# AdaLN's second and third parts in branch B's product and wo's, and key pages loaded ahead of q's loop

## The chip, the cores and the metric

The kernel runs on one core of one Trainium2 chip. Its metric is the device time of one launch in microseconds. Of the kernel before there are three timed runs and one execution that was profiled.

## The reference, cut to what matters

One layer of a decoder for a prompt of 512 tokens and 8 samples with one token each, with D = 1024, 16 heads, and a past of 1024 positions a sample in pages of 128 (float32 throughout):

```python
sh1, sc1, g1, sh2, sc2, g2 = split(silu(c) @ ada_w + ada_b, 6)     # adaLN
h = rms_norm(x, norm1_g) * (1.0 + sc1) + sh1
xr, gr, q, k, v, fl, ga, gb = split(h @ w_in)
ya = (rg_lru(causal_dwconv(xr)) * gelu(gr)) @ w_proj_a             # branch A
yb = attend(q, k, v, log_sigmoid(fl + b_f)) @ w_proj_b             # branch B
x = x + g1 * ((sigmoid(ga) * ya + sigmoid(gb) * yb) @ w_o)
h2 = rms_norm(x, norm2_g) * (1.0 + sc2) + sh2
x = x + g2 * ((silu(h2 @ w_gate) * (h2 @ w_up)) @ w_ffn_out)
y = rms_norm(x, normf_g)
```

For a sample, `attend` takes the logits of q against the keys of its own pages, adds the sums of the logarithms of the forget gates between the two positions, and takes a softmax over past and present together. The page table gives each sample's pages; the product with the keys is what the change moves the loads of. `ada_w` is 1024 x 6144, 24 MB, and its six outputs are needed at different times: sh1 and sc1 for h, g1 only after wo, sh2 and sc2 for h2, g2 at the end.

## The kernel before, in words

Tokens lie along the free dimension (520 columns: 512 of the prompt, 8 samples), in two halves of 260; features lie on the partitions in eight tiles of 128. A product of 128 outputs runs over eight tiles of the inputs, and each step is three matmuls: high part of the weights by high part of the input, low by high, high by low. So a half of a product is 24 matmuls and a whole one 48.

Weights come through `wraw` (two buffers of 1 MB, loaded by SyncE in `load_chunks`, 256 columns at a time), and `split_upto` makes their high part on ScalarE (`whi`, L246) and their low part on VectorE (`wlo`, L248), three buffers of each. `begin()` opens a product: it calls `tick`, loads chunks and splits weights some products ahead. `tick` runs the work on the samples' past: it sums key pages (`key_sum`), and issues the loads of the next ones (`key_pages`, as many as the table `KEYS` says for that product). Each engine runs its instructions in a fixed order, which a list scheduler chose; `tc.issue_after` puts one instruction behind another.

A key page for the first samples comes in halves. `key_halves` takes one buffer of the pool `pgp` (seven buffers, shared with AdaLN's weights and the value pages) and has GpSimd issue two loads of 256 KB (`page_load`, L698, each with a read of the page table before it at L697, and at least four loads behind the last). The row of q by which the page is multiplied (`qb`, L715) is broadcast by another load from GpSimd; it comes from `qtd`, which ScalarE stores after the first four products of q were transposed. `key_sum` is a multiply (L742) and a reduce (L743) on VectorE.

AdaLN is computed in three parts. The first (scale and shift of h) is done at the start. The second (g1, sh2) and the third (sc2, g2) are each made of eight pieces, one for each tile of the inputs: `ada_load` (L350 and following; two loads of 512 KB, `araw`) and `ada_piece` (four matmuls at L370 with 32 output columns each, in the four column groups of the array). `ada_copy` takes the sum out of the bank, and `ada_end` transposes it (four transposes at L382) and adds the bias on VectorE.

The order of the stages: AdaLN's first part and h; q's loop (eight products; before the change a piece of AdaLN's second part follows each but the first); the RG-LRU loop (xr, gates A and B, gr, with the eighth piece); k, v and the prompt's attention; branch A's product (pa); branch B's product in the merge loop (pb), into which the table `ADA2` puts four pieces of the third part; wo by halves (`wo_done`, four more pieces in its first half); then the FFN. Before wo's product SyncE also loads x again (L100) and, tile by tile, the sigmoids and branch A (`sB`, `tA`), which are added and multiplied to `mix`. In q's loop there are further the past's forget gates: `past_load` gathers them, `past_turn` transposes them (eight transposes) and sums them on GpSimd (L451 to L454); and the weights of the RG-LRU's gates are split (`gate_split`, L909 and L910).

Of the kernel before, what the change touches and what calls it, by code (L numbers as in the profile page):

```python
# [12 lines left out]
ALU = mybir.AluOpType  # L13
# [5 lines left out]
NP = 512  # L19
NS = 8  # L20
# [45 lines left out]
def kernel(ctx, tc, xT, par, gates, b_f, cst, cse, own, cache_k, cache_v, cache_lf, pt,  # L66
# [13 lines left out]
    def slot(name, cols=NT, dt=F32, parts=128):  # L80
        return heap.tile([parts, cols], dt, name=name, tag="slot")
# [108 lines left out]
    def flush():  # L190
        while stores:
# [1 line left out]

    later = {}

    KEYS = dict(zip(range(42), (2, 2, 1, 0, 2, 2, 2, 2, 1, 1, 1, 1, 2, 2, 2, 1, 0, 1, 0, 1, 2, 2, 2, 2, 1, 1, 1, 1, 2, 2, 1, 2,
                                1, 1, 1, 2, 1, 1, 1, 1, 2, 0)))
    VALUES = (19, 21, 23, 25, 27, 29, 31, 35, 37, 39)
    LAST_POOL = 41
# [152 lines left out]
    def ada_load(which, kq):  # L352
        if kq >= KT:
            return
        for g2 in range(2):
            raw = pgp.tile([128, 2, 512], F32, name="araw", tag="pg")
            c0 = which * 2048 + g2 * 1024
            sp.dma_start(raw, ada_w[kq * 128:kq * 128 + 128, c0:c0 + 1024].rearrange("p (g c) -> p g c", g=2))
            ada_raw.setdefault((which, kq), []).append(raw)
# [13 lines left out]
    def ada_copy(which):  # L373
        sb = slot("adas", 512)
        act.copy(sb, ada_acc[which])
        ada_acc[which] = sb
# [54 lines left out]
    def past_load():  # L431
        t = wp.tile([NS * NPAGE, 2048], F32, name="lfp", tag="wraw", bufs=2)
        pool.indirect_dma_start(out=t, out_offset=None, in_=cache_lf,
                                in_offset=bass.IndirectOffsetOnAxis(ap=idx[:, 0:1], axis=0),
                                bounds_check=NPOOL - 1)
        lfp.append(t.rearrange("p (k h) -> p h k", h=H))
# [70 lines left out]
    def first_h(f):  # L507
        t, hi, lo = slot("hr"), slot("hh", dt=F32R), slot("hl", dt=F32R)
        a_, b_ = amp1[:, f, 0:1], mod[:, 0, f, 0:1]
        act.activation(hi[:, :NP], xn[f][:, :NP], AF.Identity, scale=a_, bias=b_)  # L510
        pool.tensor_tensor(t[:, NP:], xn[f][:, NP:], amp1[:, f, 1:9], ALU.mult)
        pool.tensor_tensor(t[:, NP:], t[:, NP:], mod[:, 0, f, 1:9], ALU.add)
        dve.tensor_scalar(t[:, :NP], xn[f][:, :NP], a_, b_, ALU.mult, ALU.add)
        act.copy(hi[:, NP:], t[:, NP:])
        dve.tensor_tensor(lo, t, hi.bitcast(F32), ALU.subtract)
        h.append((hi, lo))
# [76 lines left out]
    q_weights(1, raw, 4, 2)  # L593
    raw = wraw()
    q_weights(1, raw, 0, 4)
    for n in range(3):
        ada_load(1, n)
    load_chunks(0)
    sp.dma_start(cs[:, C_TRI:], cst[:, C_TRI:])

# [33 lines left out]
    def forget_logits(w):  # L634
        part, fl = slot("flp", parts=2 * H), slot("fl", parts=H)
        for j, (t0, t1) in enumerate(HALVES):
            b = bank(f"pfl{j}")
            for k in range(KT):
                for m in range(2):
                    pe.matmul(b[:2 * H, :HALF], lhsT=w[:, k], rhs=h[k][m][:, t0:t1],  # L640
                              start=k == 0 and m == 0, stop=k == KT - 1 and m == 1)
            act.copy(part[:, t0:t1], b[:2 * H, :HALF])

        def close():
            for j, (t0, t1) in enumerate(HALVES):
                b = bank(f"pfs{j}")
                pe.matmul(b[:H, :HALF], lhsT=cs[:2 * H, C_S16:C_S16 + H], rhs=part[:, t0:t1], start=True, stop=True)
                act.activation(fl[:, t0:t1], b[:H, :HALF], AF.Identity, bias=bf)
            sp.dma_start(fld, fl)

        return close
# [55 lines left out]
    def key_halves(s, j, half):  # L707
        if not S:
            S.extend(slot("S", 512) for _ in range(2))
        pg = pgp.tile([128, 2, 512], F32, name="pg", tag="pg")  # L710
        for a in range(2):
            page_load(cache_k, s, j + a, pg[:, a], 512 * half, 512 * half + 512)
        if j == 0:
            t = slot("qb", 512)
            pool.dma_start(t, qtd[s:s + 1, 512 * half:512 * half + 512].partition_broadcast(128))  # L715
            qb[0] = t
        pend.append([0, s, j, pg, qb[0], half])

    def key_page(s, j, half=None):
# [155 lines left out]
    q8 = keep.tile([128, KT * NS], F32, name="q8")  # L875

    def q_done(i, t):
        pool.tensor_copy(q8[:, NS * i:NS * i + NS], t[:, NP:])
        sp.dma_start(qd[i], t)
        pe.transpose(qtp[i // 4][:, 128 * (i % 4):128 * (i % 4) + 128], t[:, NP:], ident)  # L880
        if i % 4 == 3:
            q_samples(i // 4)
# [30 lines left out]
    for i in range(KT):  # L913
        if i % 4 == 0:
            qtp.append(bank(f"qt{i}", NS))
        if i < 6:
            t = qpart[i]
            for j, (t0, t1) in enumerate(HALVES):
                b = bank(f"q{i}_{j}")
                for k in range(4):  # L920
                    q_matmuls(1, i, j, k, b)
                dve.tensor_tensor(t[:, t0:t1], b[:, :HALF], t[:, t0:t1], ALU.add)
        else:
            t = slot("q")
            product(f"q{i}", h, to(t, act.copy))
        if ready:
            q_done(*ready.pop())
        ready.append((i, t))
        if i == 2:
            flw = forget_weights()  # L930
        if i == 3:
            split_upto(0)
            for n in range(KT):
                gate_load(n)
        if i >= 4:
            for n in (2 * i - 8, 2 * i - 7):
                gate_split(n)
        if i == 4:
            past_load()
            split_upto(1)  # L940
            with tc.issue_after(state["last"].ins), tc.issue_after(state["act"].ins):
                decay()
                past_conv()
            close = forget_logits(flw)
        if i == 6:
            close()
            past_turn(0)
        if i == 7:
            past_turn(1)
        if i:  # L950
            ada_piece(1, i - 1)
            if i < 5:
                ada_load(1, i + 2)
        if i == 3:
            q_done(*ready.pop())
        if i == 5:
            tick(2, 0)
    q_last = ready.pop()


# [105 lines left out]
    for i in range(0, KT, 2):  # L1066
        conv(i)
        if i == 0:
            q_done(*q_last)
        else:  # L1070
            if i == 2:
                ada_piece(1, 7)
                ada_copy(1)
            both(lru_root, i - 2)
            gelu(i - 2)
            lru_scan(i - 2)
        conv(i + 1)
        if i:
            gelu(i - 1)
            lru_scan(i - 1)  # L1080
            if i < 6:
                both(lru_mul, i - 2)
                both(lru_g, i - 2)
        if i < 6:
            gate_a(i)
            if i:
                lru_gates(i)
            gate_a(i + 1)
            if i == 2:
                ada_end(1)  # L1090
            lru_gates(i + 1 if i else 0)
            gate_b(i)
            if i == 0:
                lru_gates(1)
                past_sums(0)
            gate_b(i + 1)
            if i == 0:
                past_sums(1)
                ada_load(1, 7)
            both(lru_exp, i)  # L1100
            if i == 2:
                log_forget()
            if i == 4:
                sum_forget()
        else:
            lru_gates(i)
            with tc.issue_after(state["gate"].ins):
                both(lru_mul, i - 2)
                both(lru_g, i - 2)
                split_upto(state["n"] + 2)  # L1110
            gate_a(i)
            lru_gates(i + 1)
            gate_a(i + 1)
            both(lru_exp, i)
            gelu(i)
            both(lru_root, i)
            gelu(i + 1)
            both(lru_scan, i)
            both(lru_mul, i)
            both(lru_g, i)  # L1120
# [317 lines left out]
        dve.tensor_tensor(t, t, u, ALU.add)  # L1438
        mix[i] = split("mix", t)

    ADA2 = [(0,), (), (1,), (), (2,), (), (3,), (), (4,), (5,), (6,), (7,), (), (), (), ()]
    for i in range(KT):
        if i == 6:
            load_x()
        if i + 1 < KT:
            merge_load(i + 1)
        merge(i)
        for n in ADA2[i]:
            ada_piece(2, n)
    amp2 = []  # L1450


# [67 lines left out]
                    split_upto(u + KT + i)  # L1520

    def wo_done(i, j, b):
        for n in ADA2[KT + i] if j == 0 else ():
            ada_piece(2, n)
            if n == KT - 1:
                ada_copy(2)
        if i == 6 and j == 0:
            ada_end(2)
            amp2.append(amplitude("n2", 4, P_N2))
        residual(i, b, 2, j)  # L1530
        sum_squares("sq2", i, ss2, x[i], j, pool if i < 6 else dve)
# [243 lines left out]
```

## Time and profile before

| | us |
|---|---|
| three runs, median (lowest, highest) | 1024.76 (1024.56, 1027.04) |
| the profiled execution | 1028.43 |
| its span, first to last instruction | 1026.5 |
| TensorE busy in it | 998.2 |
| VectorE busy | 797.3 |
| ScalarE busy | 548.3 |
| GpSimd busy | 323.9 |

The span is what the profile shows of one execution; the time has a little around it (1.9 us here). Busy shares are means over stages with different limits, so what counts is, at each place, which engine is waited for. Rows of the timeline begin with the start in us and the duration; a duration of a matmul is modelled, so the distance between starts is what a matmul costs. `x8` at the end of a row counts records. In brackets stands how long the engine idled before the row and what it waited for. A name with a q behind the engine (SPq) is the issuing of a transfer.

### The profile page before, as it was taken

The numbers are of one execution on the slowest core, as the hardware profiler recorded it, in microseconds if no ns is written. First come the engines' busy times: TensorE is split into PE (matmuls) and PEld (weight loads), VectorE is DVE, ScalarE is ACT, GpSimd is POOL, SyncE is SP. The second block draws the span as 40 slices with busy tenths as digits, with TensorE's granted clock in tenths as the row PEclk, the third lists the DMA queues.
The fourth block names the chain that finished last, engine by engine and source line by source line (L and its number), as shares of the span: only waits on it lengthen the run. The fifth ranks groups of instructions, "written<-read, shape, count | busy, mean of one in ns | idle before, by whom it ended". The sixth has DMA issues, their size and how long they took to land.

```text
span 1026.5 us, 21287 instructions
## 1 busy us (share of the span) xinstructions
PE 998.2 (97%) x8012; PEld 922.6 (90%) x8012; DVE 797.3 (78%) x1423; ACT 548.3 (53%) x1128; POOL 323.9 (32%) x416
## 2 busy tenths in 40 slices
PE   5999899999999999999999999999999999999996
PEld 2788889999999988887888989999999999999996
DVE  5555899997999978887666544868888888888864
ACT  4532565866673267777876223554444444445453
POOL 0314420112134235464430001493442433425212
PEclk9999899999999999999999999999999999999999
DMA  9988986878988999899675784324243242333122
GB/s 324 349 271 292 302 272 188 267 199 279 283 288 279 322 314 311 278 298 279 187 251 192 252 305 134 84 63 124 63 124 106 80 124 80 86 103 104 62 63 84
DMA packets 164377, 206.97 MB, mean 202 GB/s; under 512 B 9890, under 2 KB 125106, under 8 KB 164210
## 3 DMA queue, kind: packets, MB, share of 16 engines
q1 hardware_dynamic: 147554, 152.52, 48.1%
q0 software_dynamic: 13040, 46.67, 13.6%
q10 hardware_dynamic: 3680, 6.42, 1.7%
q8 instruction: 63, 1.03, 0.4%
q14 instruction: 40, 0.33, 0.1%
HBM read 192.49 MB, written 13.09 MB: 200 GB/s over the span
## 4 chain that ended last, share of the span: by engine, by line
PE 86%; DVE 6%; ACT 2%; DMA 2%; issue 1%; POOL 1%; SPq 0%; POOLq 0%; DVEq 0%; ACTq 0%
PE fo L305 12%; PE gb L305 5%; PE wo L305 5%; PE ga L305 5%; PE pb L305 4%; PE k L305 4%; PE v L305 4%; PE gr L305 3%; PE xr L305 3%; PE pa L305 3%; PE pv L835 3%; PE po L1292 2%; PE qp L538 2%; PE q L538 2%; PE ada L370 1%; PE fi L305 1%
## 5 line engine op out<-in xcount | busy, mean ns | idle before, releaser
L246 ACT CAST whi<-wraw 128x1024 fp32r<-128x1024 f32 (+1 forms) x79 | 82.0, 1039 | 115.6 <-PE pb L305 34.9
L248 DVE TENSOR_TENSOR wlo<-wraw,whi 128x1024 fp32r<-128x1024 f32 (+1 forms) x79 | 99.2, 1256 | 21.2 <-ACT whi L246 18.8
L270 ACT CAST wb<-ws 128x512 fp32r<-128x512 f32 x72 | 44.8, 622 | 92.5 <-PE fo L305 64.6
L305 PE MATMUL fo<-ach,wb 128*128 128x260 f32 x512 | 93.5, 282 | 0.0
L698 POOL DMA_DIRECT2D pg<-in_cache_k_dram x74 | 39.5, 533 | 151.8 <-DVE S L747 75.2
L305 PEld LDWEIGHTS fo<-ach,wb 128*128 128x128 f32 x512 | 79.0, 188 | 0.0
L271 DVE TENSOR_TENSOR wb<-wraw,wb 128x512 fp32r<-128x512 f32 x86 | 74.4, 865 | 5.7 <-ACT wb L270 4.7
L261 POOL TENSOR_TENSOR ws<-wraw 128x512 f32<-128x512 f32 x18 | 24.7, 1374 | 157.6 <-DMA wraw<-in_w_fi_dram 90.9
L271 DVE TENSOR_TENSOR wb<-ws,wb 128x512 fp32r<-128x512 f32 x72 | 63.8, 887 | 13.4 <-ACT wb L270 11.6
L305 PE MATMUL fo<-acl,wb 128*128 128x260 f32 x256 | 72.4, 283 | 0.0
L270 ACT CAST wb<-wraw 128x512 fp32r<-128x512 f32 x86 | 53.5, 622 | 33.3 <-ACT cp L1664 6.1
L746 DVE TENSOR_TENSOR pg<-pg,qb 128x1024 f32<-128x1024 f32 x48 | 57.8, 1218 | 0.0
L747 DVE TENSOR_REDUCE S<-pg 128x16 f32<-128x1024 f32 x48 | 57.5, 1208 | 0.3
L1249 POOL TENSOR_SCALAR p<-p,mu 128x128 f32<-128x128 f32 (+3 forms) x28 | 38.7, 1392 | 55.5 <-DVE mu L1245 41.2
L305 PEld LDWEIGHTS fo<-acl,wb 128*128 128x128 f32 x256 | 48.3, 189 | 0.0
L1243 ACT ACTIVATE p<-p,mu 128x128 f32<-128x128 f32 (+3 forms) x64 | 35.4, 554 | 19.6 <-DVE mu L1242 19.4
L305 PE MATMUL ga<-hh,wlo 128*128 128x260 f32 x128 | 37.6, 294 | 3.4 <-DVE wlo L248 3.4
L305 PE MATMUL v<-hh,whi 128*128 128x260 f32 x128 | 37.3, 291 | 0.8 <-ACT row L815 0.5
L305 PE MATMUL ga<-hh,whi 128*128 128x260 f32 x128 | 37.6, 294 | 0.0
L305 PE MATMUL ga<-hl,whi 128*128 128x260 f32 x128 | 37.5, 293 | 0.0
L305 PE MATMUL k<-hh,whi 128*128 128x260 f32 x128 | 37.3, 291 | 0.0
L305 PE MATMUL pb<-oh,whi 128*128 128x260 f32 x128 | 36.8, 288 | 0.3 <-ACT oh L1350 0.3
(1101 smaller groups left out, 3964.1 us busy)
## 6 DMA issues: line engine op xcount, KB each, us to landing
araw<-in_ada_w_dram SPq DMA_DIRECT2D x48, 512.0 KB, 8.1
wraw<-in_w_fi_dram SPq DMA_DIRECT2D x44, 512.0 KB, 4.3
pg<-in_cache_k_dram POOLq DMA_DIRECT2D x42, 512.0 KB, 6.1
pg<-in_cache_v_dram SPq DMA_DIRECT2D x42, 512.0 KB, 5.6
wraw<-in_w_in_dram SPq DMA_DIRECT2D x34, 512.0 KB, 7.6
wraw<-in_w_in_dram SPq DMA_DIRECT2D x11, 1024.0 KB, 9.3
pg<-in_cache_v_dram POOLq DMA_DIRECT2D x22, 512.0 KB, 6.1
pg<-in_cache_k_dram POOLq DMA_DIRECT2D x32, 256.0 KB, 5.8
```

The source lines that it names most:

```text
L246: state["act"] = act.copy(hi[:, :k1 - k0], src)
L248: state["last"] = dve.tensor_tensor(lo[:, :k1 - k0], src, hi[:, :k1 - k0].bitcast(F32), ALU.subtract)
L270: state["act"] = act.copy(t[:, :4], src)
L271: state["last"] = dve.tensor_tensor(t[:, 4:], src, t[:, :4].bitcast(F32), ALU.subtract)
L305: state["mm"] = pe.matmul(out[:, :t1 - t0], lhsT=wt[k], rhs=at, start=k == 0 and m == 0, stop=k == nk - 1 and m == 2)
L538: state["mm"] = pe.matmul(b[:, :HALF], lhsT=wt, rhs=at[:, t0:t1], start=k == 0 and m == 0, stop=k == 3 and m == 2)
L698: done.append(eng.dma_start(pg, cache[bass.ds(r, 1), :, c0:c1].rearrange("a p c -> (a p) c")))
L746: dve.tensor_tensor(pg, pg, q, ALU.mult)
L747: last = dve.tensor_reduce(S[r // 2][:, c:c + H], pg.rearrange("p (h d) -> p h d", d=DH), AX.X, ALU.add)
L835: pe.matmul(pv[0][32 * gq:32 * gq + 32, :], lhsT=pw[r][:, c:c + 32], rhs=pgs[gq // 2][:, 512 * hf:512 * hf + 512], start=j == 0, stop=j == ...
L1243: act.activation(p[:, :n + 128], p[:, :n + 128], AF.Exp, bias=mu[:, 0:1], scale=-1.0, accum_out=mu[:, 1:2])
L1249: (pool.tensor_scalar(p, p, mu[:, 2:3], None, ALU.mult) if a and i + 1 < KT else act.activation(p, p, AF.Copy, scale=mu[:, 2:3]))
```

## The change

It does five things.

1. The loads and pieces of AdaLN's second part leave q's loop and the RG-LRU loop. The table `PIECES` puts all sixteen pieces of the second and third part in a row: nine in the eight products of branch B, the first two in one place, and seven in the first half of wo. `ada_copy(1)` follows the second part's last piece, and `ada_end(1)` the merge loop.
2. The first page loads are called in q's loop: two at i = 4 and two at i = 5, instead of one at i = 5; `KEYS` loses three of them for that (the entries of its third and fifth product go down). The loads of the first pages need not wait for others: the four entries that `loads[pool]` gets are operations of h, so that the scheduler may place the loads right behind these.
3. The row of q (qb) for the first sample is called after its second page, not with the first.
4. The past is turned at i = 5, both halves in a row, in place of one half at i = 6 and one at i = 7; its load stands behind the first copy of q for the samples.
5. Four of the eight gate splits stay in q's loop (i = 5 and 6), four move into the RG-LRU loop. Chunks 1 and 2 of the weights are called at i = 4 and i = 6.

```diff
-    KEYS = dict(zip(range(42), (2, 2, 1, 0, 2, 2, 2, 2, 1, 1, 1, 1, 2, 2, 2, 1, 0, 1, 0, 1, 2, 2, 2, 2, 1, 1, 1, 1, 2, 2, 1, 2,
+    KEYS = dict(zip(range(42), (2, 2, 0, 0, 1, 2, 2, 2, 1, 1, 1, 1, 2, 2, 2, 1, 0, 1, 0, 1, 2, 2, 2, 2, 1, 1, 1, 1, 2, 2, 1, 2,
...
-        pool.tensor_tensor(t[:, NP:], t[:, NP:], mod[:, 0, f, 1:9], ALU.add)
+        state["hr"] = pool.tensor_tensor(t[:, NP:], t[:, NP:], mod[:, 0, f, 1:9], ALU.add)
...
-    for n in range(3):
-        ada_load(1, n)
     load_chunks(0)
...
         if j == 0:
-            t = slot("qb", 512)
-            pool.dma_start(t, qtd[s:s + 1, 512 * half:512 * half + 512].partition_broadcast(128))
-            qb[0] = t
+            qb[0] = slot("qb", 512)
+        if j == (2 if s == half == 0 else 0):
+            pool.dma_start(qb[0], qtd[s:s + 1, 512 * half:512 * half + 512].partition_broadcast(128))
...
-        if i >= 4:
-            for n in (2 * i - 8, 2 * i - 7):
+        if i in (5, 6):
+            for n in (2 * i - 10, 2 * i - 9):
                 gate_split(n)
         if i == 4:
-            past_load()
+            with tc.issue_after(state["q8"].ins):
+                past_load()
             split_upto(1)
+            load_chunks(1)
+            loads[pool] += [state["hr"]] * 4
+            key_pages(2)
...
+        if i == 5:
+            past_turn(0)
+            past_turn(1)
+            key_pages(2)
         if i == 6:
             close()
-            past_turn(0)
-        if i == 7:
-            past_turn(1)
-        if i:
-            ada_piece(1, i - 1)
-            if i < 5:
-                ada_load(1, i + 2)
+            load_chunks(2)
...
-        if i == 5:
-            tick(2, 0)
...
-            if i == 2:
-                ada_piece(1, 7)
-                ada_copy(1)
+            if i < 6:
+                gate_split(i + 2)
+                gate_split(i + 3)
...
-    ADA2 = [(0,), (), (1,), (), (2,), (), (3,), (), (4,), (5,), (6,), (7,), (), (), (), ()]
+    PIECES = [(0, 1), (2,), (3,), (4,), (5,), (6,), (7,), (8,), (9, 10), (11,), (12, 13), (14,), (15,), (), (), ()]
...
-        for n in ADA2[i]:
-            ada_piece(2, n)
+        for n in PIECES[i]:
+            ada_piece(1 + n // KT, n % KT)
+            if n == KT - 1:
+                ada_copy(1)
+    ada_end(1)
...
-        for n in ADA2[KT + i] if j == 0 else ():
-            ada_piece(2, n)
-            if n == KT - 1:
+        for n in PIECES[KT + i] if j == 0 else ():
+            ada_piece(2, n - KT)
+            if n == 2 * KT - 1:
                 ada_copy(2)
```

What the scheduler makes of it, at three places. VectorE, up to the low half of gate A's first weights (`wlo`; the two `wlo` rows of xr's chunk, then the one of gate A's). Before:

```order
L248 TENSOR_TENSOR wlo_1187<-wraw_1037,whi_1186 128x1024
L910 TENSOR_TENSOR gws_1245<-gw_755,gws_1245 128x256
L910 TENSOR_TENSOR gws_1248<-gw_757,gws_1248 128x256
L742 TENSOR_TENSOR pg_1142<-pg_1142,qb_1163 128x1024
L742 TENSOR_TENSOR pg_1165<-pg_1165,qb_1163 128x1024
L743 TENSOR_REDUCE S_944<-pg_1142 128x2x8
L743 TENSOR_REDUCE S_944<-pg_1165 128x2x8
L248 TENSOR_TENSOR wlo_1310<-wraw_1039,whi_1309 128x1024
```

With the change:

```order
L740 TENSOR_TENSOR pg_1028<-pg_1028,qb_1049 128x1024
L740 TENSOR_TENSOR pg_1051<-pg_1051,qb_1049 128x1024
L741 TENSOR_REDUCE S_775<-pg_1028 128x2x8
L741 TENSOR_REDUCE S_775<-pg_1051 128x2x8
L248 TENSOR_TENSOR wlo_1194<-wraw_773,whi_1193 128x1024
L740 TENSOR_TENSOR pg_1151<-pg_1151,qb_1049 128x1024
L740 TENSOR_TENSOR pg_1172<-pg_1172,qb_1049 128x1024
L741 TENSOR_REDUCE S_775<-pg_1151 128x2x8
L741 TENSOR_REDUCE S_775<-pg_1172 128x2x8
L248 TENSOR_TENSOR wlo_1266<-wraw_1072,whi_1265 128x1024
```

The split of gate A's weights (the last row of each) stood behind the sixth key sum and stands behind the eighth; the two gate splits ahead of it are gone.

GpSimd in and behind q's loop (`after` are the past's sums). Before:

```order
L698 DMA pg_1016<-in_cache_k_dram 128x512
L451 MEMSET after_1124 128x64
L452 COPY after_1124<-lk_1122 128x64
L454 TENSOR_TENSOR after_1124<-after_1124,lk_1122 128x64
L697 TENSOR_LOAD ptb_103
L697 ISA x2
L698 ISA
L698 DMA pg_1142<-in_cache_k_dram 128x512
L454 TENSOR_TENSOR after_1124<-after_1124,lk_1122 128x64 x2
```

With the change, where the twelfth load is the first row:

```order
L696 DMA pg_1051<-in_cache_k_dram 128x512
L714 DMA qb_798<-qtd_568 128x512
L876 COPY q8_583<-qp_111 128x8
L695 TENSOR_LOAD ptb_103
L695 ISA x2
L696 ISA
L696 DMA pg_1151<-in_cache_k_dram 128x512
```

Twelve loads (six buffers) now stand ahead of qb, the first of them right behind h; before, qb stood ahead of all page loads, and later ones stood between the adds of the past.

TensorE in wo's first half (`ada2` is the third part's sum). Before:

```order
L305 MATMUL wo0_0_9028<-mixh_9016,wlo_8891 128x260
L370 MATMUL ada2_8514<-araw_9053,silc_99 32x512
L305 MATMUL wo0_0_9028<-mixl_9017,whi_8890 128x260
L370 MATMUL ada2_8514<-araw_9053,silc_99 32x512
L370 MATMUL ada2_8514<-araw_9055,silc_99 32x512 x2
L305 MATMUL wo1_0_9071<-mixh_8510,whi_8959 128x260
```

With the change:

```order
L370 MATMUL ada2_8978<-araw_9029,silc_99 32x512 x2
L370 MATMUL ada2_8978<-araw_9031,silc_99 32x512 x2
L305 MATMUL wo1_0_9055<-mixh_8434,whi_8917 128x260
L305 MATMUL wo1_0_9055<-mixh_8434,wlo_8918 128x260
L305 MATMUL wo1_0_9055<-mixl_8435,whi_8917 128x260
L305 MATMUL wo1_0_9055<-mixh_8516,whi_8917 128x260
L305 MATMUL wo1_0_9055<-mixh_8516,wlo_8918 128x260
L370 MATMUL ada2_8978<-araw_9037,silc_99 32x512 x2
L305 MATMUL wo1_0_9055<-mixl_8517,whi_8917 128x260
L305 MATMUL wo1_0_9055<-mixh_8591,whi_8917 128x260
L305 MATMUL wo1_0_9055<-mixh_8591,wlo_8918 128x260
```

Before, all pieces in wo but one stood whole between two of its products. Now one is whole and the other six stand in halves (one buffer of `araw` each) with matmuls of wo between them. In branch B's product the first two pieces stand together and the other seven whole, one behind each product. Over the whole program AdaLN's second and third parts make 17 such groups on TensorE before and 21 with the change.

More of the change, by code (lines that the diff above doesn't have):

```diff
@@ L877, in q_done @@
     def q_done(i, t):
-        pool.tensor_copy(q8[:, NS * i:NS * i + NS], t[:, NP:])
+        c = pool.tensor_copy(q8[:, NS * i:NS * i + NS], t[:, NP:])
+        state.setdefault("q8", c)
         sp.dma_start(qd[i], t)
@@ L1088 @@
             gate_a(i + 1)
-            if i == 2:
-                ada_end(1)
             lru_gates(i + 1 if i else 0)
@@ L1098 @@
                 past_sums(1)
-                ada_load(1, 7)
             both(lru_exp, i)
```

## The prediction

> **What bounds the kernel now.** I read the page first (busy time by engine, then the chain of waits), and after it the table of what TensorE waited for. Columns of that table: who waits, for whom, us in total, times, longest.
>
> ```profile
> PE 998.2 (97%) x8012; PEld 922.6 (90%) x8012; DVE 797.3 (78%) x1423; ACT 548.3 (53%) x1128; POOL 323.9 (32%) x416
> PE 86%; DVE 6%; ACT 2%; DMA 2%; issue 1%; POOL 1%; SPq 0%; POOLq 0%; DVEq 0%; ACTq 0%
> ...
> PE ss L555 <- DMA x<-in_xT_dram: 10.2, 1, 10.2
> ...
> PE ga L305 <- DVE wlo L248: 3.4, 1, 3.4
> ...
> PE pa L305 <- DVE wlo L248: 0.9, 1, 0.9
> ```
>
> TensorE is busy for 97% of the span and is 86% of the chain that ends last. A change can therefore gain in two ways only: fewer instructions on TensorE, or one of its few waits gone. Between the start and the tail there is one wait of size, 3.4 us at the first product of merge gate A. The timeline of TensorE there:
>
> ```profile
> 107.43 0.28 PE L305 MATMUL xr<-hl,whi 128*128 128x260 f32 x1
> 107.55 0.31 PE L305 MATMUL ga<-hh,whi 128*128 128x260 f32 x1
> 111.25 0.58 PE L305 MATMUL ga<-hh,wlo 128*128 128x260 f32 x1 [3.40 <-DVE wlo L248]
> 111.64 0.42 PE L305 MATMUL ga<-hl,whi 128*128 128x260 f32 x1
> ...
> 117.27 0.29 PE L305 MATMUL ga<-hh,wlo 128*128 128x260 f32 x1
> ```
>
> A matmul of this shape follows its predecessor after 0.12 us (107.43 to 107.55). From 107.55 to 117.27 there are 28 steps, which is 3.4 us at that pitch, and they took 9.72. So the stall costs **6.3 us**: about 3.6 of plain waiting, the rest matmuls at about 0.22 us apiece before the fast pitch returns. On VectorE the cause stands in front of the split that the wait names:
>
> ```profile
> 86.30 1.23 DVE L742 TENSOR_TENSOR pg<-pg,qb 128x1024 f32<-128x1024 f32 x1 [8.20 <-DMA pg<-in_cache_k_dram]
> ...
> 99.89 0.75 DVE L910 TENSOR_TENSOR gws<-gw,gws 128x256 fp32r<-128x256 f32 x2
> ...
> 106.59 1.23 DVE L742 TENSOR_TENSOR pg<-pg,qb 128x1024 f32<-128x1024 f32 x1 [3.30 <-DMA pg<-in_cache_k_dram]
> 107.73 2.34 DVE L743 TENSOR_REDUCE S<-pg 128x16 f32<-128x1024 f32 x2
> 109.98 1.22 DVE L248 TENSOR_TENSOR wlo<-wraw,whi 128x1024 fp32r<-128x1024 f32 x1
> ```
>
> VectorE runs in order. A key sum waits 3.3 us for its page, and gate A's low half (109.98) stands behind it. VectorE had idled 8.2 us at 86.30 for the first page, so the same sums could have been done earlier. The page in question was issued late by GpSimd, which also had to wait for the row of q (qb):
>
> ```profile
> 71.58 0.41 ACT L909 CAST gws<-gw 128x256 fp32r<-128x256 f32 x1 [2.79 <-DMA gw<-in_gates_dram]
> 71.99 0.56 ACTq L188 DMA_DIRECT2D qtd<-qt  x1
> 73.83 0.59 POOL L715 DMA_DIRECT2D qb<-qtd  x1 [3.30 <-DMA qtd<-qt]
> ...
> 100.30 0.54 POOL L698 DMA_DIRECT2D pg<-in_cache_k_dram  x1 [0.62 <-issue]
> ```
>
> **The change, part by part.** *AdaLN's pieces.* A piece is four matmuls of 32 columns, one in each column group. Two places show its price, a whole piece in branch B's product and one that the order cut in two in wo's:
>
> ```profile
> 560.98 0.28 PE L305 MATMUL pb<-ol,whi 128*128 128x260 f32 x1
> 561.18 1.06 PE L370 MATMUL ada<-araw,silc 128*32 128x512 f32 x8
> 562.18 0.39 PE L305 MATMUL pb<-oh,whi 128*128 128x260 f32 x1
> 562.40 0.28 PE L305 MATMUL pb<-oh,wlo 128*128 128x260 f32 x1
> ...
> 608.54 0.28 PE L305 MATMUL wo<-mixh,wlo 128*128 128x260 f32 x1
> 608.76 1.04 PE L370 MATMUL ada<-araw,silc 128*32 128x512 f32 x2
> 609.73 0.39 PE L305 MATMUL wo<-mixl,whi 128*128 128x260 f32 x1
> 610.05 1.06 PE L370 MATMUL ada<-araw,silc 128*32 128x512 f32 x6
> 611.04 0.39 PE L305 MATMUL wo<-mixh,whi 128*128 128x260 f32 x1
> L370 PE MATMUL ada<-araw,silc x128: 592/605/617, 57.3 to 622.8; 128*32 128x512 f32 x128
> ```
>
> 128 records for 16 pieces of four make two records an instruction. Without the piece, the matmul at 562.40 would have come two steps after 560.98, at 561.22: a group costs **1.18 us**. The group with one instruction (608.76) needs 0.97 us to the next product, the one with three 0.99, the whole one 1.00 (561.18 to 562.18). So the price is per group, whatever is in it. What was 17 groups before (16 pieces, one of them cut) becomes 21 in the order shown above: one double group, eight whole pieces, twelve halves. For the double one I take 1.18 + 0.98 = 2.16 us, since its second four use the same column groups; not below 1.18 (if it cost as a single one) and not above 2.36. Removed early: 8 x 1.18 = 9.4. Late: from 9 x 1.18 = 10.6 to 20 x 1.18 + 2.16 = 25.8, which is 15.2 more. Net **+5.7 us** on TensorE, which nothing hides, because TensorE has no idle time at either place. If a half cost half (0.6), the twelve would be 7 us cheaper; 608.76 speaks against it, and I keep it for the range.
>
> The four transposes that end the second part (L382) move with it and cancel; the past's two turns are the same sixteen transposes put together.
>
> *The key pages and the stall.* Seven pieces are gone ahead of gate A, so its product starts at 107.55 - 7 x 1.18 = 99.3 and wants its low half then. Twelve page loads now stand on GpSimd ahead of q's row and no longer between the adds of the past's turn; they are in memory long before they are used, and qb takes the place of the page as what VectorE waits for first. The store of q's rows (71.99) stood behind a gate cast that waited 2.79 us for its weights; those casts move later, and three pieces ahead of it go, so it comes between 65.7 (earlier by 2.79 + 3 x 1.18) and 69.2 (by 2.79 alone). The broadcast qb was issued 1.84 later, between 67.5 and 71.0 now, and the answer on that tile gives its landing:
>
> ```profile
> DMA to landing us min/median/max: 5.0/6.5/8.1
> ```
>
> 5.0 to 6.5 us make it 72.5 to 77.5. From there VectorE has eight key sums to do before gate A's split, at two reduces in 2.25 us (107.73 to 109.98), so 1.13 for each multiply or reduce: 18.0; with three splits at 1.22 and four small operations like those at 99.89, 0.38 each, it is 23.2 us. Gate A's low half is ready between 95.7 and 100.7, in the middle 98. It is wanted at 99.3. I take the stall as gone: **-6.3 us**; the far end leaves a wait of 1.4 us, the bound above it is that nothing is gained.
>
> The Trainium skill ("TensorE: Matmul & The Clock Gate", Part 1, the table of the two states) says that the clock falls to half after one idle window of about 3.4 us and returns after about as long a busy one. The trace agrees: after the gap of 3.6 us the pitch doubled for some 6 us, after the 0.9 us wait at pa it did not. By that rule a wait that only shrinks also loses the slow matmuls, so even a remaining 2 us would cost 2 and not 6.3.
>
> *Their loads.* Sixteen loads of half a megabyte leave the stage around q's loop and come in around branch B's product and wo's. The table by stages shows how full the queues were; its columns after the stretch and its length are TensorE, its loads, VectorE, ScalarE, GpSimd busy, granted clock, DMA share, GB/s.
>
> ```profile
> 51.40:86.00 34.60, 34.60 (x278) 28.09 (x276) 16.33 (x55) 10.43 (x25) 7.08 (x14) 1.00 0.89 299
> 86.00:111.00 25.00, 21.86 (x179) 19.60 (x178) 19.25 (x19) 10.67 (x24) 13.87 (x31) 0.99 0.88 285
> 554.00:606.00 52.00, 51.68 (x421) 47.42 (x422) 27.21 (x50) 14.26 (x26) 1.29 (x1) 1.00 0.76 262
> 590.00:596.00 6.00, 6.00 (x52) 6.00 (x52) 2.93 (x5) 1.69 (x2) 0.00 (x0) 1.00 1.03 365
> 596.00:602.00 6.00, 6.00 (x51) 5.03 (x50) 3.55 (x6) 1.67 (x2) 0.00 (x0) 1.00 1.04 390
> ```
>
> SyncE issues them in order with everything else of that stage:
>
> ```profile
> 590.00 9.03 SPq L100 DMA_DIRECT2D x<-in_xT_dram  x8
> ...
> 601.58 0.38 SPq L210 DMA_DIRECT2D wraw<-in_w_o_dram  x1
> 602.06 9.39 SPq L358 DMA_DIRECT2D araw<-in_ada_w_dram  x3
> 612.97 0.38 SPq L210 DMA_DIRECT2D wraw<-in_w_o_dram  x1
> ...
> 604.69 0.43 DVE L1436 TENSOR_TENSOR sB<-pb,sB 128x260 f32<-128x260 f32 x1 [2.53 <-DMA sB<-sBd]
> ```
>
> From 554 to 606 the core moved 52 x 262 = 13.6 MB, about 8 AdaLN loads of 0.52 MB among it. Seven buffers are full at 554 in both kernels, and in the new order 17 stand ahead of wo's last chunk, 9 x 0.52 = 4.7 MB on top: 18.3 MB in 52 + 5.7 + 1.2 = 58.9 us. That needs 311 GB/s where the queues reached 365 to 390. I take it as hidden, **0**. Without that cover it is rival A. The four gate splits moved from q's loop to the RG-LRU's (0.38 us each on VectorE) are wanted only there and cost nothing on TensorE, which the table of waits shows waiting for no such split; uncovered they would be 1.5 us.
>
> **Sum.** +5.7 - 6.3 = -0.6 us. The profiled execution took 1028.43 us with a span of 1026.5, so it would take 1027.8; the median of the three runs before is 3.7 us lower, 1024.76, and by the same difference the new one is **1024.2**.
>
> **The rivals.** *A, slower: the transfers around wo are late.* Rows 590 and 596 show the queues full already, the sum of sB at 604.69 already waits 2.5 us for a transfer, and eight x loads, more AdaLN loads and wo's third chunk now share one queue. Against it: seven buffers of lead, and no wait on TensorE there before. It decides once the reachable rate falls below 311 GB/s. At the 299 GB/s of the first row, 18.3 MB take 61.2 us, 2.3 late; at 262 they take 69.8, 11 late. In the middle, some 4 us with 2.5 more for the slow matmuls behind a wait that long: 1024.2 + 4 to 6.5, about **1030**.
>
> *B, slower: the early stall stays.* Eight sums stand ahead of gate A's split, two more than before, and all of them start with one row of q that is now issued behind page loads. If that row lands after about 80, the wait is again over 3.4 us and everything is paid: 1024.76 + 5.7 = **1030.5**. For it: 95.7 to 100.7 against 99.3 is narrow. Against it: a miss of 1 us costs about that.
>
> *C, faster: the halves are cheap.* If two instructions in a group cost 0.6, it is 7 us less, about **1017**; the second wait, 0.9 us at pa, could go besides. Against it stands 608.76, a single instruction at nearly the full price.
>
> **How the numbers follow.** Forecast 0.55 (its own range 1021.5 to 1027.5), A 0.17, B 0.14, C 0.14. About 0.3%, or 3.1 us, is what a measurement of this kernel can tell from no change. The forecast lies within it but for a tail of 0.04 on either side; C is faster; A and B are slower but for 0.03 of their mild forms. That gives faster 0.18, same 0.50, slower 0.32. To leave out no more than 2 in 10 the range takes in A and B up to 1030.5, and of C the part where the halves are a third cheaper (12 x 0.4 = 4.7): 1019.5.
>
> **What would show it.** In the new profile the table of waits should have no ga entry over 1 us and no half pitch near 100; the first multiply of a key page should wait for qb and stand near 75; gate A should begin near 99.3 in a row without a bracket. Each of the twelve halves should push the next wo matmul by about 1.18 us; if the pair costs 0.6, C is right. In wo, a bracket with araw or mix behind a matmul would be A, a bracket with wlo at ga B. A net change of TensorE's work away from +5.7 would make the sum wrong even with the stall gone.

## The result and the profile after

| | before | with the change |
|---|---|---|
| median of the runs shown with the result, us (six each) | 1027.05 (1024.56 to 1029.28) | 1035.56 (1032.39 to 1038.76) |
| ratio with its 95% interval | | 1.0085 (1.0056 to 1.0114) |
| profiled execution, us | 1028.43 | 1032.73 |
| its span, us | 1026.5 | 1031.1 |

The change made the kernel 0.85% slower, 8.5 us by the medians, and the measured time lies outside the forecast's range. The two profiled executions are only 4.3 us apart; the last point of the part on why the prediction was wrong takes up the rest.

The new profile's table of what TensorE waited for (who, for whom, us in total, times, longest):

```profile
PE ss L555 <- DMA x<-in_xT_dram: 10.0, 1, 10.0
PE qt L879 <- DVE qp L921: 2.5, 2, 1.7
PE xr L305 <- DVE wlo L248: 2.1, 2, 1.8
PE fi L305 <- DVE h2l L1499: 1.1, 2, 0.8
```

Gate A's entry of 3.4 us is gone, as forecast, but gate A does not begin near 99.3. Two entries stand in its place, and both are earlier in the program: q's transposes (qt) and xr's first two products, which come right before gate A. The timeline of TensorE at the three largest of these gaps, and at gate A:

```profile
62.65 0.28 PE L538 MATMUL q<-hl,whi 128*128 128x260 f32 x1
64.66 0.27 PE L879 MATMUL qt<-cs,qp 128*8 128x128 f32 x1 [1.73 <-DVE qp L921]
...
82.37 0.28 PE L305 MATMUL q<-hl,whi 128*128 128x260 f32 x1
83.46 0.27 PE L879 MATMUL qt<-cs,qp 128*8 128x128 f32 x1 [0.81 <-DVE qp L921]
...
90.52 0.37 PE L305 MATMUL xr<-hh,whi 128*128 128x260 f32 x1
92.66 0.39 PE L305 MATMUL xr<-hh,wlo 128*128 128x260 f32 x1 [1.77 <-DVE wlo L248]
...
93.17 0.42 PE L305 MATMUL xr<-hh,wlo 128*128 128x260 f32 x1
93.38 0.42 PE L305 MATMUL xr<-hl,whi 128*128 128x260 f32 x1
...
106.34 0.28 PE L305 MATMUL ga<-hh,whi 128*128 128x260 f32 x1
106.46 0.28 PE L305 MATMUL ga<-hh,wlo 128*128 128x260 f32 x1
```

Measured against the normal pitch the gaps cost 1.9, 1.0 and 2.0 us, a fourth one at xr's second product 0.5, and the 15 matmuls from 93.2 on that follow each other after 0.22 in place of 0.12 us another 1.5. That is 6.9 us of new cost ahead of gate A, where 6.3 went. The table by stages shows the slow stretch as a granted clock of 0.51 (columns: stretch, its length, TensorE, its loads, VectorE, ScalarE, GpSimd, clock, DMA share, GB/s):

```profile
91.00:93.00 2.00, 0.34 (x2) 0.34 (x3) 2.00 (x3) 1.02 (x2) 2.00 (x3) 1.00 0.67 226
93.00:96.40 3.40, 3.40 (x18) 3.40 (x17) 3.40 (x5) 0.52 (x2) 2.88 (x7) 0.51 0.66 217
```

What was late there is read engine by engine. First the load of the weights of q's last two products (chunk 0), from the timelines of SyncE, GpSimd, ScalarE and VectorE:

```profile
50.20 0.74 POOL L696 DMA_DIRECT2D pg<-in_cache_k_dram  x1 [1.08 <-PE qp L538]
...
52.75 0.39 SPq L210 DMA_DIRECT2D wraw<-in_w_in_dram  x1
...
61.62 1.05 ACT L246 CAST whi<-wraw 128x1024 fp32r<-128x1024 f32 x1 [7.94 <-DMA wraw<-in_w_in_dram]
...
62.70 1.23 DVE L248 TENSOR_TENSOR wlo<-wraw,whi 128x1024 fp32r<-128x1024 f32 x1 [5.29 <-ACT whi L246]
63.85 1.43 DVE L921 TENSOR_TENSOR qp<-q,qp 128x260 f32<-128x260 f32 x4
```

Chunk 0 took 8.9 us from its issue to the cast that waited for it. Seven of the early page loads were issued between 50.2 and 60.6. VectorE idled for 5.3 us before the split of that chunk, and four additions that end q's products (63.85) stood behind the split; the transpose at 64.66 waits for one of them. Behind these transposes comes the row of q, on ScalarE its store and on GpSimd its broadcast:

```profile
69.03 0.56 ACTq L188 DMA_DIRECT2D qtd<-qt  x1
...
74.00 0.54 POOL L714 DMA_DIRECT2D qb<-qtd  x1 [1.76 <-DMA qtd<-qt]
```

GpSimd, done with the page loads ahead of it, still idled 1.76 us for the store to land, so the broadcast was issued 4.97 us behind it. Then VectorE up to gate A's split:

```profile
80.15 1.23 DVE L740 TENSOR_TENSOR pg<-pg,qb 128x1024 f32<-128x1024 f32 x1 [5.35 <-DMA qb<-qtd]
...
88.27 1.21 DVE L741 TENSOR_REDUCE S<-pg 128x16 f32<-128x1024 f32 x1
...
89.82 1.43 DVE L740 TENSOR_TENSOR pg<-pg,qb 128x1024 f32<-128x1024 f32 x1
91.18 1.43 DVE L248 TENSOR_TENSOR wlo<-wraw,whi 128x1024 fp32r<-128x1024 f32 x1
...
105.00 1.21 DVE L248 TENSOR_TENSOR wlo<-wraw,whi 128x1024 fp32r<-128x1024 f32 x1
```

The first key sum waits for the row of q until 80.15. Four multiplies and three reduces stand between that and xr's first split at 91.18, whose product TensorE had begun at 90.52. The last row is gate A's split. It ends at 106.2, and the first matmul that needs it starts at 106.46. VectorE shows no idle time between 80.15 and there, so at the forecast's 99.3 gate A would have waited 6.9 us. Its wait was not removed but paid earlier, at q and xr.

In wo the pieces in halves look as the forecast said. TensorE there:

```profile
605.06 0.28 PE L305 MATMUL wo<-mixh,wlo 128*128 128x260 f32 x1
605.27 1.05 PE L370 MATMUL ada<-araw,silc 128*32 128x512 f32 x4
606.25 0.39 PE L305 MATMUL wo<-mixl,whi 128*128 128x260 f32 x1
606.48 0.28 PE L305 MATMUL wo<-mixh,whi 128*128 128x260 f32 x1
```

Four records are two instructions. From 605.06 to 606.48 lie 1.42 us, of which two normal steps are 0.24: a half costs 1.18 us, like a whole piece.

By stages, from the starts of the same matmuls in both profiles (before, after, difference):

| stretch | before | after | difference |
|---|---|---|---|
| start to branch A's first product | 313.74 | 304.57 | -9.2 |
| to branch B's first product | 240.58 | 237.99 | -2.6 |
| to the first sum of squares' product behind wo (branch B and wo) | 83.96 | 99.93 | +16.0 |
| to the end of the span | 388.2 | 388.6 | +0.4 |

The second row is k, v and the attention, which the change does not touch; e2 below, whose code is that of the kernel before there, needs 237.6 us for it. So the profiled execution of before was some 3 us slow in a place that has nothing to do with the change. Over all profiles of this document that row lies between 237.6 and 241.1.

### The profile page after: what moved, and what is told of

Read it like the earlier page. It is cut to its first block, busy times and chain, and to the rows that moved or that the text cites. A ratio compares the mean times of both kernels' runs of the same rounds, so it can differ in the third digit from the quotient of the medians.

```text
span 1031.1 us, 21277 instructions
## 1 busy us (share of the span) xinstructions
PE 1003.5 (97%) x8012; PEld 923.6 (90%) x8012; DVE 794.0 (77%) x1423; ACT 548.5 (53%) x1128; POOL 325.1 (32%) x416
## 4 chain that ended last, share of the span: by engine, by line
PE 89%; DMA 4%; DVE 3%; ACT 1%; issue 1%; POOL 1%; SPq 0%; DVEq 0%; POOLq 0%; ACTq 0%
PE fo L305 12%; PE wo L305 5%; PE k L305 5%; PE gb L305 5%; PE gr L305 5%; PE pb L305 5%; PE ga L305 5%; PE v L305 4%; PE xr L305 4%; PE pv L833 3%; PE pa L305 3%; PE ada L370 2%; PE po L1288 2%; PE qp L538 2%; PE ptt L1254 2%; PE fi L305 1%
## 5 line engine op out<-in xcount | busy, mean ns | idle before, releaser
L271 DVE TENSOR_TENSOR wb<-wraw,wb 128x512 fp32r<-128x512 f32 x86 | 76.6, 891 | 5.7 <-ACT wb L270 4.5
L271 DVE TENSOR_TENSOR wb<-ws,wb 128x512 fp32r<-128x512 f32 x72 | 59.6, 828 | 14.8 <-ACT wb L270 13.0
L1245 POOL TENSOR_SCALAR p<-p,mu 128x128 f32<-128x128 f32 (+3 forms) x28 | 38.7, 1393 | 51.7 <-DVE mu L1241 45.6
L305 PE MATMUL xr<-hh,wlo 128*128 128x260 f32 x128 | 37.1, 290 | 2.1 <-DVE wlo L248 2.1
L305 PE MATMUL xr<-hh,whi 128*128 128x260 f32 x128 | 37.4, 292 | 0.0
L305 PE MATMUL gb<-hh,whi 128*128 128x260 f32 x128 | 37.0, 289 | 0.0
```

The lines of the kernel that those rows point to most:

```text
L271: state["last"] = dve.tensor_tensor(t[:, 4:], src, t[:, :4].bitcast(F32), ALU.subtract)
L305: state["mm"] = pe.matmul(out[:, :t1 - t0], lhsT=wt[k], rhs=at, start=k == 0 and m == 0, stop=k == nk - 1 and m == 2)
L1245: (pool.tensor_scalar(p, p, mu[:, 2:3], None, ALU.mult) if a and i + 1 < KT else act.activation(p, p, AF.Copy, scale=mu[:, 2:3]))
```

## The experiments

Two theories of the early waits were put against each other. *Transfers*: page loads that start right behind h delay chunk 0 and the first row of q. *Order*: VectorE's order puts key sums ahead of xr's first split. The late part had a rival too, that a half of a piece costs half. Ratios are to the runs of the kernel before on the same chip.

**e1, pieces whole in wo.** On the changed kernel:

```diff
-        for g2, raw in enumerate(ada_raw.pop((which, kq))):
+        for g2, raw in reversed(list(enumerate(ada_raw.pop((which, kq))))):
```

The matmuls of the buffer that arrives last stand first, so that nothing separates them from the others: 15 groups in place of 21.

> The changed kernel with one edit: a piece takes its second buffer's matmuls first, so the six pieces that stood in halves in wo stand whole (15 groups in place of 21). If a group costs 1.18 us whatever is in it: 6 x 1.18 = 7.1 us less than the changed kernel, so about 1.4 us over the kernel before. Rival, a half costs half: no change, still 8.5 over the kernel before. The early waits stay as they are in both.

Measured: 1028.73 us, 1.0022 (1.0001 to 1.0043), against 1.0094 (1.0074 to 1.0113) for the changed kernel on the same chip (e4). That is 0.72%, 7.4 us, for six groups: 1.2 us each. In the profiles the way from wo's first product to the first sum of squares' product is 35.1 us in place of 42.1, again 1.2 a group. The price is per group, and the rival falls.

**e2, everything but AdaLN's move**, and **e3, AdaLN's move alone.** e2 is the changed kernel with the pieces put back to where they were; e3 is the kernel before with `PIECES` and without the pieces and loads in q's and the RG-LRU loop. From e2's edit:

```diff
-    PIECES = [(0, 1), (2,), (3,), (4,), (5,), (6,), (7,), (8,), (9, 10), (11,), (12, 13), (14,), (15,), (), (), ()]
+    PIECES = [(8,), (), (9,), (), (10,), (), (11,), (), (12,), (13,), (14,), (15,), (), (), (), ()]
...
+        if i:
+            ada_piece(1, i - 1)
+            if i < 5:
+                ada_load(1, i + 2)
```

> Everything of the change but AdaLN's move: its pieces are in q's loop, in the RG-LRU loop and every second product again. Theory (the pieces in q's loop gave the transfers and VectorE time, and taking them away made the new waits): the wait at gate A goes, no new one comes, about 6.3 us less than the kernel before. Rival (the twelve early page loads delay the weights and the row of q): waits of 1 to 2 us in q's loop come here too, no gain or a loss of a few us.

> AdaLN's move alone, with key pages, past and gate splits as in the kernel before. Theory: TensorE comes to gate A 8 us earlier but VectorE's key sums do not, so the wait grows by most of the 9.4 us that the pieces took, and the 15.2 us of the late pieces are paid in full: 10 to 15 us over the kernel before. Rival (the move itself is sound, the pages spoil it): about 5.7 over the kernel before or less.

e2: 1025.72 us, 1.0001 (0.9981 to 1.0021). e3: 1029.86 us, 1.0050 (1.0033 to 1.0068). In both the theory's number was wrong. In e2 the rival's number came, but not for its reason: there is no wait in q's loop, and the old wait is still there. Its table of waits, and GpSimd's timeline:

```profile
PE ga L305 <- DVE wlo L248: 3.6, 1, 3.6
```

```profile
71.54 1.14 POOL L698 DMA_DIRECT2D pg<-in_cache_k_dram  x2 [0.68 <-DMA qd<-qp]
75.18 1.12 POOL L698 DMA_DIRECT2D pg<-in_cache_k_dram  x2 [2.49 <-PE ada L370]
```

The first page load starts at 71.5 in spite of the change's edits, and the next one waits 2.5 us for a piece of AdaLN, whose loads hold the buffers. In e3, without those edits, the seven buffers are free and GpSimd's timeline has page loads among h's last operations; VectorE makes xr's first split with two multiplies and one reduce ahead of it:

```profile
46.74 0.55 POOL L696 DMA_DIRECT2D pg<-in_cache_k_dram  x1 [0.96 <-issue]
```

```profile
82.75 1.22 DVE L248 TENSOR_TENSOR wlo<-wraw,whi 128x1024 fp32r<-128x1024 f32 x1
```

No wait is left at gate A nor at xr (0.9 and 0.6 us are left in q's loop), which is the rival's line. Gate A's split ended at 100.1 there, ahead of gate A at 101.58, and branch A's first product began at 299.75, 14.0 us earlier than before. So it is AdaLN's move that removes the old stall; the edits on the key pages add 0.44% (e4 less e3; the two intervals leave about 0.3% either way) and bring the waits at xr.

**e4, the change once more**, without an edit.

> The changed kernel once more, for a second profile: the time of its runs went from 1032 to 1039. If the early waits are what varies, their sum differs from the 5.4 us of the first profile by about as much as the time does. Rival: the early stage repeats within 0.5 us and the difference lies in the attention or at the start.

1034.01 us (1031.03 to 1036.55). The profiled one, 1031.03, has gaps of 2.4, 2.0 and 2.0 us at the same three places (qt, and xr's two products), 6.4 in all where the first profile had 5.4, but no slow matmul behind any, so that the early cost is 6.4 us there and was 6.9. Neither line is borne out by this run alone.

**e5, page loads later**, and **e6, key sums later.** Each is the changed kernel with one edit:

```diff
+        state["q8l"] = c
...
-            loads[pool] += [state["hr"]] * 4
+            loads[pool] += [state["q8l"]] * 4
```

```diff
-        state["age"] = 1 if state["n"] < 5 else 2
+        state["age"] = 2
```

> The changed kernel with the first page loads behind the fourth copy of q on GpSimd in place of right behind h, so that none of them runs while chunk 0 of the weights and the first rows of q are moved. Theory 1 (the early page loads delay the weights and the row of q): chunk 0 lands some 3 us sooner, the waits of 1.9 us at q's transposes and of 2 us at xr's first product go, with the slow matmuls behind it: 4 to 6 us less than the changed kernel. Theory 2 (VectorE's order is at fault, with key sums ahead of xr's first split): at most the 1.9 us goes, and as the first page now lands later the wait at xr stays or grows: 0 to 2 us less. Against the kernel before: theory 1 +3 to +5, theory 2 +7 to +9.

> The changed kernel with the key sums of the first products one product later, so that VectorE makes xr's first split ahead of them; the loads stay where the change has them. Theory 2: the waits at xr (2.0 and 0.5 us) and the 1.5 us of slow matmuls behind them go, the 1.9 us at q's transposes stays: about 4 us less than the changed kernel, +5 against the kernel before, if gate A does not wait in their place. Theory 1: the split is late for its weights and not for the sums, nothing changes, +9.

e5: 1030.49 us, 1.0050 (1.0028 to 1.0072). Chunk 0 is there 5.3 us after its issue, the wait at q's transposes is gone, and xr's gaps are 1.6 and 1.0 us with no slow matmuls. ScalarE, GpSimd and VectorE in its profile:

```profile
57.30 1.05 ACT L246 CAST whi<-wraw 128x1024 fp32r<-128x1024 f32 x1 [4.39 <-DMA wraw<-in_w_in_dram]
...
64.43 0.55 ACTq L188 DMA_DIRECT2D qtd<-qt  x1
```

```profile
68.52 0.54 POOL L714 DMA_DIRECT2D qb<-qtd  x1
```

```profile
75.96 1.23 DVE L740 TENSOR_TENSOR pg<-pg,qb 128x1024 f32<-128x1024 f32 x1 [4.38 <-DMA qb<-qtd]
```

The row of q comes 4.2 us earlier than in the changed kernel, though the pages come later. Its own way is no shorter: from store to first use it took 11.5 us here, where page loads run beside it as well, and 11.1 in the changed kernel. It comes earlier because the store is issued 4.6 us earlier. The gate weights' loads of SyncE stand beside chunk 0 in both, so they alone do not delay it. The theory of transfers holds for chunk 0 and through it for the row, at 0.44% or 4.5 us by the ratios (0.3% either way); the waits at xr, which it also said would go, only shrank.

e6: 1031.95 us, 1.0052 (1.0032 to 1.0072). The waits at xr are gone and none came at gate A: the theory of order holds as well, at 4.3 us (0.3% either way). Its profiled execution, the slowest of its ten, is a weak witness for that, since a longer wait ahead of xr gave VectorE time; e8, with the same edit and without that wait, has none at xr either, but some at gate A. The longer wait shows how late chunk 0 can come; TensorE and ScalarE:

```profile
68.80 0.37 PE L879 MATMUL qt<-cs,qp 128*8 128x128 f32 x1 [6.20 <-DVE qp L921]
```

```profile
65.76 1.99 ACT L246 CAST whi<-wraw 128x1024 fp32r<-128x1024 f32 x2 [12.42 <-DMA wraw<-in_w_in_dram]
```

Chunk 0 took 13.3 us here with the same loads beside it as in the changed kernel (8.9, 9.4, and 9.2 in e1). Over all profiles the two groups do not overlap: 5.3 to 5.4 us in e5, e8, e9 and e10, whose page loads start later, and no more than that in before and e2 (where the cast, 5.3 and 5.4 after the issue, waits for something else); 8.4 to 13.3 in the changed kernel, e1, e3, e4, e6 and e7.

**e7, AdaLN's move alone, pieces whole**, and **e8, the change with the edits of e1, e5 and e6.**

> AdaLN's move alone (as in e3) with its pieces whole in wo (as in e1). If the two simply add: 0.50% - 0.72% of the kernel before, about 2 us less than it. If the early stage or the transfers around wo depend on where the loads are taken up: no less than the kernel before.

> The changed kernel with the edits of e1, e5 and e6 together. By either theory no early wait over 1 us is left and the groups are 15: early -15.7 us as forecast, late +15.2 - 7.1 = 8.1, so about 7 us less than the kernel before. If a new wait comes at gate A because the sums are later: as the kernel before or slower.

e7: 1022.74 us, 0.9963 (0.9948 to 0.9979): faster than the kernel before, and the sum of the two edits (0.50% - 0.72% = -0.22%) lies at the edge of that interval. e8: 1022.56 us, 0.9970 (0.9957 to 0.9983), 3.1 us less where 7 were expected: with the sums later, three waits of 1.8 to 1.9 us stand at products of gate A, two for weights and a later one for `st` (L791, a maximum in the past's softmax). Its waits:

```profile
PE ga L305 <- DVE wlo L248: 3.3, 2, 1.7
PE ga L305 <- DVE st L791: 1.7, 1, 1.7
```

**e9, e7 with the page loads behind the fourth copy of q**, and **e10, the change with the edits of e1 and e5.**

> As e7 (AdaLN's move alone, pieces whole), with the first page loads behind the fourth copy of q as in e5. In e7's profile two waits are left early, 1.7 us at q's first product (h's last operations stand between page loads on GpSimd) and 1.7 us at q's transposes (chunk 0 landed 9.3 us after its issue). Theory: both go, chunk 0 lands within 5.5 us, 3.4 us less than e7: 0.6 to 0.7% less than the kernel before. Rival (the later pages make the key sums late): a wait at xr or gate A takes their place, as e7 or slower.

> The changed kernel with the edits of e1 and e5 together. If they add: 0.50% - 0.72%, about 0.2% less than the kernel before. If the remaining waits at xr (1.6 and 1.0 us in e5) grow: as the kernel before.

e9: 1021.45 us, 0.9967 (0.9951 to 0.9983). In its profile no wait over 0.5 us in all is left between the sums of squares at the start and the FFN's first product (the top of its table of waits):

```profile
PE ss L555 <- DMA x<-in_xT_dram: 9.9, 1, 9.9
PE fi L305 <- DVE h2l L1492: 1.0, 2, 0.8
PE ss L555 <- DVE sq L550: 0.7, 1, 0.7
PE v L305 <- ACT row L813: 0.5, 2, 0.3
```

Both waits of e7 went as expected, yet the ratio is that of e7 within the intervals. The two profiles show the gain: from q's first product to xr's 36.9 us in place of 40.2. They also show 1.0 us lost again between products of gates A and B, and a start of q that is 1.2 us later in e9 (it lies between 49.8 and 51.7 over all profiles). Whether that holds for the other executions is open. e10: 1023.46 us, 0.9982 (0.9964 to 1.0000), as if the edits add; in its profile xr's second product waits 3.7 us, since its split (97.33) stands behind key sums that waited 1.0 us for a row of q and 1.2 us for a page. Both causes are still at work there.

## Why the prediction was wrong

- **What bounds the kernel**: right. TensorE is 97% busy before and after, and what changed the time is groups on it and its waits.
- **A group costs 1.18 us whatever is in it**: right, on the row of a single instruction. Halves took 1.18 us in the new profile and e1 gives 1.2 a group. Rival C falls with it.
- **Late part, +15.2 us**: right. Branch B and wo together take 16.0 us more in the profile, with four transposes moved there.
- **The transfers around wo are hidden (0)**: right. There is no wait for araw, mix or sB on TensorE in those stages. Rival A did not happen.
- **The wait at gate A goes, -6.3 us**: it is gone from the table, but not as the text had it. In the changed kernel gate A's split was ready at 106.2, outside the text's "between 95.7 and 100.7", and found nothing waiting only because TensorE came at 106.34. AdaLN's move alone does remove it (e3). The text credited the page loads; e2 has these edits and keeps the wait. By e2 and e3 what decides is AdaLN's move, which leaves the seven buffers free for the page loads; the buffers alone were not tried.
- **The step that failed** is the working from the row of q to gate A's split, and that only this one deadline was checked. The store at 69.03 is still within the text's 65.7 to 69.2. The broadcast followed after 4.97 us, where 1.84 had been carried over from the profile before, in which the queues were less full (mean DMA share 0.70 meanwhile, now 1.04). Its landing, 6.1 us, is within the 5.0 to 6.5 taken, though the line used has 8.1 as its longest. So the row was used at 80.15 and not "72.5 to 77.5", and VectorE then needed 26.1 us in place of 23.2.
- **The deadlines left out**: with pieces gone every deadline ahead of gate A comes forward too: q's transposes, and xr's first split, wanted at 95.84 - 8.3, about 87.6. From the text's own row of q at 72.5 to 77.5, the 11.0 us that VectorE took from 80.15 to 91.18 and 1.2 for the split end at 84.7 to 89.7, so the deadline lies in the middle of the range, with no slack. The order of VectorE shown ahead of the prediction has only xr's second split, so the first was not seen there.
- **The loads counted as free**: "they are in memory long before they are used" is true of the pages, but they ran beside chunk 0 (8.9 us in place of about 5.3), on which q's transposes hang by VectorE's order, and on these the row of q. New waits and slow matmuls of 6.9 us took the place of the 6.3: the early part gave -9.2 us where the forecast has -9.4 - 6.3 = -15.7.
- **The clock.** From the idle window in the Trainium skill ("TensorE: Matmul & The Clock Gate", Part 1) the text concluded that a wait that only shrinks also loses the slow matmuls. The gap of 2.1 us at 90.52 was followed by 15 of them. The same part of the Trainium skill says that the window is free-running, and that fits what the runs show of like gaps, some with and some without; the step to "2 us would cost 2" was the text's own, and wrong.
- **Rival B** had the right sign, and its condition came true: the row of q was used just after 80. It put the whole wait at gate A, where in fact it fell on q and xr, and its 5.7 us over the kernel before are less than the 8.5 measured.
- **The size.** In the profiles the account closes: -9.2 early, +16.0 late, +0.4, which is +7.2, against an execution like e2's (1025.68 us in all, 7.05 less than the changed kernel's 1032.73). The forecast was made against an execution that was 3 us slow in the attention, and its correction by the medians of three runs kept that out. The medians' further 1.3 us fit executions with a longer wait for chunk 0, like e6's, or with more slow stretches; none of the changed kernel's profiles shows such an execution, so this is argued and not shown.

## What to carry to other kernels

When work leaves a stage that its engine bounds, every deadline behind it comes forward: check the first load, the first split and the first row that follow, not only the stall that one means to remove. A load that is made early for its own sake competes with the one that is due next, so give it a start behind that one, and put small work that runs in order (here key sums) behind the split that is wanted first, as far as the next split leaves room (e8's did not). Where an operation's price is per group, keep groups whole: taking the later buffer's matmuls first did that in one line, and with AdaLN's move alone gave a kernel 0.37% (0.21 to 0.52) faster than the one before.

## What the runs showed of the hardware that had not been expected

A gap on TensorE of a little over 2 us was followed by some 15 matmuls at half the clock in three cases (2.1 us in the changed kernel, 2.3 and 2.2 in e1, about 1.5 us each) and by none in five (2.0 in the changed kernel; 2.5, 2.1 and 2.2 in e4; 2.0 in e8), so the length alone does not decide. Nor does it decide how many: after the 3.70 and 3.85 us of before and e2 it was 26 matmuls, after 4.0 us in e10 about 22, and after the 6.5 us of e6 about 12, with the fast pitch back 2.8 us after the gap. In e1's profile the table by stages for one with and in e4's for one without:

```profile
100.60:104.00 3.40, 3.40 (x16) 3.40 (x17) 3.40 (x4) 0.29 (x1) 1.81 (x5) 0.51 0.79 236
```

```profile
64.40:68.00 3.60, 3.60 (x31) 3.42 (x32) 2.40 (x5) 0.74 (x3) 1.39 (x5) 1.00 1.03 366
```

And a load of 1 MB that was issued among seven loads of 256 KB from another engine's queue took 8.4 to 13.3 us in place of 5.3. In the changed kernel the queues had been all but empty just before, as the table by stages shows (DMA share 0.05), since nothing had been issued for that time:

```profile
46.00:52.00 6.00, 6.00 (x53) 6.00 (x52) 5.37 (x10) 4.80 (x14) 4.09 (x10) 1.00 0.05 10
52.00:58.00 6.00, 6.00 (x53) 5.98 (x52) 3.72 (x7) 1.68 (x4) 3.04 (x6) 1.00 0.87 266
58.00:64.00 6.00, 4.93 (x42) 4.70 (x40) 1.30 (x2) 2.08 (x2) 1.10 (x2) 1.00 1.02 296
```

The store of the row of q, only 16 KB, shows it as well. In six profiles GpSimd waited for it, and the broadcast followed 1.8 us after the store in before (mean DMA share 0.70 meanwhile), 2.8 and 2.7 us in e3 and e7 (0.82 and 0.79), 4.1 in e10 (0.89), 5.0 in the changed kernel and in e1 (1.04 and 1.05).
